# Preparing the second four row tiles over blocks 3 to 7, reordering block 0, and moving one tile pool

## The chip, the cores and the metric

The kernel runs on one core of a Trainium2 chip. The metric is device time in microseconds, as the median of several runs of the whole program. Matrix products run on TensorE (PE in the profile, with PEld for its weight loads), elementwise work on VectorE (DVE), ScalarE (ACT) and GpSimd (POOL); SyncE (SP) issues nearly all DMA transfers. Each engine works through its own list of instructions in order.

## The reference, cut to what matters

One layer of a diffusion backbone: 1024 latent tokens of width 1024 and 256 context tokens, in float32. The inputs are normalised and modulated, multiplied with one combined input matrix of seven blocks of 512 columns, run through retention and differential attention, an output projection and a gated MLP with a depthwise convolution.

```python
m_lat = sc @ w_mod[l] + b_mod[l]                        # 6 x 1024 modulation values
h_lat = rms_norm(x, norm1_g[l]) * (1.0 + sc1) + sh1     # (1024, 1024)
h_ctx = rms_norm(ctx, norm1_g[l]) * (1.0 + csc1) + csh1 # (256, 1024)
... = split_heads(h_lat @ w_in, ...)                    # 7 blocks of 512 columns
...
u = h2 @ w_up ; a, b = split(conv3(u)) ; x = x + g2 * ((silu(a) * b) @ w_down)
return rms_norm(x, final_g)
```

What the change touches is the first part (h_lat, and h_lat times the last 512 columns of w_in), and the place in memory of one tile pool in the product with w_down.

## The kernel before, in words

Tokens are cut into row tiles of 128: eight of the latents (x) and two of the context. Every float32 product is made of three: each operand is split into a high part (rounded) and a low part (the rest), and `passes` (L129 to L134) multiplies high by high (L132), high by low (L133) and low by high (L134).

The first stage (L500 to L718) works on the last block of w_in while its own operands are still being made. The latents are needed transposed and modulated, as hT: for each of eight blocks of 128 columns (d or k = 0 to 7) `modulate` (L544) transposes four row tiles into one PSUM tile (L548), lets ACT write the high part of hT (L551), DVE the exact value (L553) and DVE (even d) or POOL (odd d) the low part (L555). Before that, each row tile has to be loaded (`load_row`, L578), its squares summed on ACT (`square`, L534, L536), the sum raised to the power -1/2 by a small DVE step (L114) and a POOL step (L115) in `power` (L538), and the tile scaled on DVE (`scale`, L541). The modulation values of block d come from w_mod: two pieces of 512 KB are loaded (`mod_load`, five buffers, L512), multiplied on PE (`mod_part`, L520), copied as a row by ACT (`mod_row`, L524) and turned by PE and DVE (`mod_sums`, L530 to L532). The slices of w_in are loaded by `w_load` and split by `w_split` into a high part on ACT (L575) and a low part on DVE (L576). `turn_over(n)` (L591) makes n throw-away products of 128 columns, each two PE instructions, whose result nobody reads.

The rows 0 to 3 (xs0) make the first half of hT, the rows 4 to 7 (xs1) the second. The loop over k (L637) multiplies block k for the row tiles 0 to 3, the first two and the last two apart (`part_products`, L587), and puts the preparation of block k + 2 between. In the kernel before, the second row tiles are loaded in blocks 2 to 5, squared and scaled in blocks 3 to 5, and their latents made in blocks 6 and 7 and at the start of row tile 4. Behind the loop come the stores of row tiles 0 and 1 (`store_to`, two buffers, L394 to L403), and the row tiles 4 and 5 (L712), with the context's preparation put in by `between` (L694). `in_order` (L120, called in L718) fixes the order, as written in the program, of all instructions of PE, DVE, ACT and SP between `begin` and that line. Instructions outside, such as the loads of the rope table (L731) and of the next weights (L186), may be moved in between by the scheduler.

The last stage (from L1330) multiplies the gated hidden tiles (`ghl`, made from stored rows by ACT in L1346 and DVE in L1347) with w_down, whose pieces stay in `resident` tiles (W). The pools of ghl (dop, two buffers of 8 KB a partition) and of the final rows (fin) take memory at the right side, that of W (wres) at the left; memory is reused tile by tile: a new tile waits for the last reader of each old tile that it overlaps. The right side held the tiles of the convolution (`up` in L1204), whose last ones are stored by `down_operands` (L1216; L1220 to L1232, on POOL's queue for the last two blocks). The left side held yT, the operands of the MLP's first product.

Of the kernel before, what the change touches and what calls it, by code (L numbers as in the profile page):

```python
# [17 lines left out]
P = 128  # L18
D = 1024
KD = D // P  # L20
# [52 lines left out]
def kernel(  # L73
# [16 lines left out]
    nc = tc.nc  # L90
    mm = nc.tensor.matmul
# [63 lines left out]
    with ExitStack() as p1:  # L155
# [19 lines left out]

        hT = [[hp.tile([P, KD, 512], F32R, name=f"hT{a}{i}") for i in range(2)] for a in range(2)]
        xs0 = [xr.tile([P, D], F32, name=f"xs{t}") for t in range(4)]
        cT = []
        sm = hp.tile([P, 16], F32, name="sm")
        mcol = hp.tile([P, KD, 2, 2], F32, name="mcol")  # L180
# [33 lines left out]
        def lat_lhs(t, k):  # L214
            return tuple(hT[a][t // 4][:, k, (t % 4) * P : (t % 4 + 1) * P] for a in range(2))
# [284 lines left out]
        with ExitStack() as p0:  # L500
# [61 lines left out]
            def wget(k, c0, c1):  # L562
                return tuple(t[:, k % 2, c0:c1] for t in sl[k // 2])
# [12 lines left out]
                nc.vector.tensor_tensor(out=lo, in0=raw, in1=r32(hi), op=ALU.subtract)  # L576

            def load_row(t):  # L578
                nc.sync.dma_start(out=xs0[t] if t < 4 else xs1[t - 4], in_=x[t * P : (t + 1) * P, :])

            def latents(half, d):
                modulate((xs0, xs1)[half], d, 0, hT[0][half][:, d, :], hT[1][half][:, d, :])
# [2 lines left out]
                modulate(xc, d, 1, cT[0][:, d, :], cT[1][:, d, :])  # L585

            def part_products(ts, k):  # L587
                for t in ts:
                    passes(part[t], lat_lhs(t, k), wget(k, 0, 512), k == 0, k == KD - 1)

            def turn_over(n):  # L591
                for _ in range(n):
# [2 lines left out]
            store = store_to(dv_row, c0=NTC)  # L595
            begin = len(nc.cur_bb.bb.instructions)
            mod_load(0, 0)
            for t in range(3):
                load_row(t)
            mod_load(0, 1)  # L600
            load_row(3)
            w_load(0, 2)
            for q in range(2):
                mod_load(1, q)
            mod_load(2, 0)
            turn_over(4)
            mod_part(0, 0)
            turn_over(10)
            square(xs0[0], 2)
            square(xs0[1], 3)  # L610
            power(2)
# [4 lines left out]
            mod_load(2, 1)  # L616
            w_load(1)
            turn_over(2)
            mod_row(0)
            power(4)  # L620
            scale(xs0[1], 3)
            square(xs0[3], 5)
            mod_sums(0)
            turn_over(4)
            scale(xs0[2], 4)
            power(5)
            w_split(0, 1)
            scale(xs0[3], 5, 0, 2 * P)
            latents(0, 0)
            mod_part(1, 0)  # L630
            mod_part(1, 1)
# [5 lines left out]
            for k in range(KD):  # L637
                part_products((0, 1), k)
                if k == 0:
                    mod_sums(1)  # L640
                    latents(0, 1)
                if k < 2:
                    for q in range(2):
                        mod_part(k + 2, q)
                    mod_row(k + 2)
                if k == 7:
                    latents(1, 2)
                    latents(1, 3)
                if 1 < k < 6:
                    load_row(k + 2)  # L650
                n = k + 4
                if n < KD:
                    for q in range(2):
                        mod_load(n, q)
                if k in (0, 2):
                    w_load(2 + k // 2)
                part_products((2, 3), k)
                if k + 2 < KD:
                    mod_sums(k + 2)
                    latents(0, k + 2)  # L660
                    if 0 < k < 5:
                        for q in range(2):
                            mod_part(k + 3, q)
                        mod_row(k + 3)
                if k in (0, 2, 4):
                    w_split()
                if k == 3:
                    square(xs1[0], 6)
                    power(6)
                if k == 4:  # L670
                    square(xs1[1], 7)
                    scale(xs1[0], 6)
                    power(7)
                if k == 5:
                    first.close()
                    cp = pctx.enter_context(tc.tile_pool(name="cp", bufs=1, side="right"))
                    cT.extend(cp.tile([P, KD, LC], F32R, name=f"cT{a}") for a in range(2))
                    for t in range(NTC):
                        xc.append(xp.tile([P, D], F32, name="xc", tag="wt", bufs=5))
                        nc.sync.dma_start(out=xc[t], in_=ctxt[t * P : (t + 1) * P, :])  # L680
                    square(xs1[2], 8)
                    scale(xs1[1], 7)
                    power(8)
                    square(xs1[3], 9)
                    scale(xs1[2], 8)
                    power(9)
                    scale(xs1[3], 9)
                if k >= 6:
                    latents(1, 4 * (k - 6))
                    latents(1, 4 * (k - 6) + 1)  # L690
            for t in range(2):
                store(t, part[t])

            def between(t, k):  # L694
                if (t, k) == (4, 0):
                    latents(1, 6)
                    latents(1, 7)
                if (t, k) == (4, 1):
                    for i in (2, 3):
                        store(i, part[i])  # L700
# [27 lines left out]

        m2p = m2c.enter_context(tc.tile_pool(name="m2p", bufs=1))
        pad(m2p, 128)  # L730
        rtab = load_rope(1)  # L731
        natural(wget, lat_lhs, range(6, NT), store)
        natural(wget, ctx_lhs, range(NTC), store_to(dv_row))
        wg = stream_block(5)
# [593 lines left out]
    ctx_ya.close()  # L1328

    with ExitStack() as p5:  # L1330
        dop = p5.enter_context(tc.tile_pool(name="dop", bufs=2, side="right", reuse_waits="tile"))
        fin = p5.enter_context(tc.tile_pool(name="fin", bufs=1, side="right", reuse_waits="tile"))
        wres = p5.enter_context(tc.tile_pool(name="wres", bufs=1, reuse_waits="tile"))

# [275 lines left out]
```

## Time and profile before

| | us |
|---|---|
| median of 3 runs | 1405.5 |
| the runs | 1404.98, 1409.08, 1405.5 |
| the profiled execution | 1403.12 |
| its span in the trace | 1401.4 |
| PE busy in the span | 1366.3 (97%) |
| DVE, ACT, POOL busy | 999.9, 729.3, 298.3 |
| DMA moved | 218.81 MB, 156 GB/s |

How to read the rows that follow. A row of the timeline, or of the chain that ended last, has the start in us from the span's start, the duration, the engine, the line of the kernel, the operation, the tile written and those read, the shape and a count of merged instructions; in brackets how long the engine stood before it, and what ended that. Matmuls overlap each other, so the time that one costs is read from start to start. A row of the waits has the total in us, how often and the longest. A row of the windows has the stretch, the busy time and number of instructions of PE, PEld, DVE, ACT and POOL, the clock granted to TensorE (1.00 is full speed), the busy share of the DMA engines and GB/s. A row of the groups has the busy time, the mean of one in ns and the idle time before. Loads issued by SP have no own wait in the chain; a row "DMA xs<-x" is the time from issue to landing.

### The profile page before, as it was taken

The numbers are of one execution on the slowest core, as the hardware profiler recorded it, in microseconds if no ns is written. First come the engines' busy times: TensorE is split into PE (matmuls) and PEld (weight loads), VectorE is DVE, ScalarE is ACT, GpSimd is POOL, SyncE is SP. The second block draws the span as 40 slices with busy tenths as digits, with TensorE's granted clock in tenths as the row PEclk, the third lists the DMA queues.
The fourth block names the chain that finished last, engine by engine and source line by source line (L and its number), as shares of the span: only waits on it lengthen the run. The fifth ranks groups of instructions, "written<-read, shape, count | busy, mean of one in ns | idle before, by whom it ended". The sixth has DMA issues, their size and how long they took to land.

```text
span 1401.4 us, 19449 instructions
## 1 busy us (share of the span) xinstructions
PE 1366.3 (97%) x7040; PEld 1148.0 (82%) x7040; DVE 999.9 (71%) x1458; ACT 729.3 (52%) x1394; POOL 298.3 (21%) x321
## 2 busy tenths in 40 slices
PE   8899999999999899999999999999999999999997
PEld 5688888887887799998888788888888888788886
DVE  3655864423686798896347997887778877699757
ACT  3553313333565589997126655555445555455543
POOL 1310000001556133421201732223332220000001
PEclk9999999999999999999999999999999999999999
DMA  9545885465575696641421223322323325963523
GB/s 337 224 154 196 291 273 190 132 186 174 161 248 154 179 221 156 126 98 46 166 83 60 91 106 113 113 97 106 112 99 113 103 75 180 344 240 101 183 91 127
DMA packets 96807, 218.81 MB, mean 156 GB/s; under 512 B 9220, under 2 KB 31236, under 8 KB 96200
## 3 DMA queue, kind: packets, MB, share of 16 engines
q1 hardware_dynamic: 88408, 192.41, 40.3%
q0 software_dynamic: 8160, 24.91, 7.8%
q8 instruction: 55, 0.90, 0.3%
q14 instruction: 40, 0.33, 0.1%
q10 hardware_dynamic: 144, 0.26, 0.0%
HBM read 160.13 MB, written 57.41 MB: 155 GB/s over the span
## 4 chain that ended last, share of the span: by engine, by line
PE 82%; DVE 7%; DMA 4%; issue 3%; POOL 2%; ACT 2%; SPq 0%; POOLq 0%; ACTq 0%; DVEq 0%
PE chain L132 5%; PE chain L133 5%; PE chain L134 5%; PE pv L872 5%; PE pA L840 5%; PE c L134 4%; PE c L132 4%; PE c L133 4%; PE pn L132 4%; PE pn L134 4%; PE pn L133 4%; PE pl L134 3%; PE third L132 3%; PE third L133 3%; PE pl L132 3%; PE third L134 3%
## 5 line engine op out<-in xcount | busy, mean ns | idle before, releaser
L132 PE MATMUL pl<-hT,whi 128*128 128x512 f32 x256 | 106.2, 415 | 0.0
L132 PE MATMUL chain<-T,whi 128*128 128x512 f32 x264 | 103.2, 392 | 0.8 <-ACT ua L1156 0.5
L133 PE MATMUL chain<-T,whi 128*128 128x512 f32 x264 | 102.8, 389 | 0.0
L134 PE MATMUL chain<-T,wlo 128*128 128x512 f32 x264 | 102.4, 389 | 0.0
L134 PE MATMUL pl<-hT,wlo 128*128 128x512 f32 x256 | 100.3, 392 | 0.1
L133 PE MATMUL pl<-hT,whi 128*128 128x512 f32 x256 | 100.0, 391 | 0.0
L843 DVE TENSOR_REDUCE mt<-pA 128x1 f32<-128x1280 f32 x64 | 95.2, 1490 | 3.7 <-PE pA L840 3.3
L840 PE MATMUL pA<-ks,qhl 128*128 128x512 f32 (+1 forms) x384 | 89.5, 369 | 3.2 <-ACT p L847 3.0
L132 PE MATMUL c<-whi,ghl 128*128 128x512 f32 x232 | 90.4, 390 | 1.4 <-ACT ghl L1346 1.4
L134 PE MATMUL c<-whi,ghl 128*128 128x512 f32 x232 | 90.4, 390 | 0.5 <-DVE ghl L1347 0.5
L133 PE MATMUL c<-wlo,ghl 128*128 128x512 f32 x232 | 90.3, 389 | 0.0
L847 ACT ACTIVATE p<-pA,mt 128x1280 f32<-128x1280 f32 x64 | 85.5, 1335 | 6.7 <-DVE mt L843 6.7
L1011 ACT CAST whi<-cmb 128x512 fp32r<-128x512 f32 x62 | 38.5, 622 | 81.2 <-PE chain L133 60.7
L840 PEld LDWEIGHTS pA<-ks,qhl 128*128 128x128 f32 x384 | 67.6, 189 | 15.5 <-ACT p L847 3.7
L132 PE MATMUL pn<-whi,hT 128*128 128x512 f32 x192 | 79.1, 412 | 0.0
L872 PE MATMUL pv<-va,aT 128*128 128x128 f32 x640 | 77.0, 275 | 0.1
L134 PE MATMUL pn<-whi,hT 128*128 128x512 f32 x192 | 75.6, 394 | 0.9 <-POOL hT L555 0.5
L133 PE MATMUL pn<-wlo,hT 128*128 128x512 f32 x192 | 75.4, 393 | 0.0
L1014 DVE TENSOR_TENSOR wlo<-cmb,whi 128x512 fp32r<-128x512 f32 x62 | 60.5, 976 | 20.3 <-ACT whi L1011 20.3
L872 PEld LDWEIGHTS pv<-va,aT 128*128 128x128 f32 x640 | 74.0, 192 | 0.7 <-DVE yT L901 0.3
L1170 POOL TENSOR_TENSOR cmb<-wrb 128x512 f32<-128x512 f32 x19 | 27.1, 1426 | 221.9 <-DMA wrb<-w_up 159.1
L1011 ACT CAST whi<-wra 128x512 fp32r<-128x512 f32 x55 | 33.7, 622 | 72.9 <-PE third L133 42.6
(313 smaller groups left out, 3819.2 us busy)
## 6 DMA issues: line engine op xcount, KB each, us to landing
wm<-w_mod SPq DMA_DIRECT2D x32, 512.0 KB, 5.3
raw<-w_in SPq DMA_DIRECT2D x27, 512.0 KB, 4.7
wra<-w_up SPq DMA_DIRECT2D x24, 512.0 KB, 3.3
wrb<-w_up SPq DMA_DIRECT2D x22, 512.0 KB, 3.5
W<-w_down SPq DMA_DIRECT2D x44, 256.0 KB, 6.2
ad<-s SPq DMA_DIRECT2D x20, 512.0 KB, 3.4
wra<-ad SPq DMA_DIRECT2D x20, 512.0 KB, 3.4
kvs<-kvg SPq DMA_DIRECT2D x36, 256.0 KB, 3.1
```

Source lines behind the costliest of these rows:

```text
L132: mm(ps, lh, rh, start=first, stop=False, skip_group_check=more)
L133: mm(ps, lh, rl, start=False, stop=False, skip_group_check=more)
L134: mm(ps, ll, rh, start=False, stop=last, skip_group_check=more)
L840: mm(self.pa[m][:, c0:c1], self.q[:, m, i, qs], self.k[:, m, c0:c1], start=(i == 0), stop=(i == 1))
L843: nc.vector.tensor_reduce(out=self.mt[:, m : m + 1], in_=self.pa[m][:, :LK], axis=AX.X, op=ALU.min)
L847: nc.scalar.activation(self.p[m], self.pa[m][:, :LK], AF.Exp, scale=-1.0, bias=self.mt[:, m : m + 1], accum_out=self.s[:, m : m + 1])
L872: mm(self.pv, self.aT[:, c, :], self.v[:, c, :], start=(c == 0), stop=(c == NKT - 1))
L1011: cast = nc.scalar.copy(hi, src)
L1014: nc.vector.tensor_tensor(out=lo, in0=src, in1=r32(hi), op=ALU.subtract)
L1170: nc.gpsimd.tensor_tensor(out=s1, in0=b1, in1=b2, op=ALU.add)
```

## The change

Five things are changed.

1. The loads of the row tiles 0 to 3 are issued by ACT at the very start, instead of by SP between the loads of w_mod.
2. At the start, `turn_over(10)` goes and `turn_over(4)` behind the first `mod_sums` becomes `turn_over(6)`; `mod_row(0)` moves behind the fourth square, the third tile's scaling ahead of `mod_sums(0)`, and the first weight split behind the fourth tile's scaling.
3. In block 0 the third products (low by high) of all four row tiles come behind the first two of all.
4. The second row tiles are loaded in blocks 1 to 4 (ahead of the w_mod pieces of the block), squared in blocks 3 and 4 (ahead of that block's weight split) and scaled in blocks 4 and 5; the latents of the second half are all made in blocks 6 and 7. The rope table's load is put into the fixed order, behind the loop.
5. The pool of ghl moves to the left side, so that W's pool lies behind it and the final rows' pool begins where ghl lay.

```diff
@@ -175,6 +175,8 @@
 
         hT = [[hp.tile([P, KD, 512], F32R, name=f"hT{a}{i}") for i in range(2)] for a in range(2)]
         xs0 = [xr.tile([P, D], F32, name=f"xs{t}") for t in range(4)]
+        for t in range(4):
+            nc.scalar.dma_start(out=xs0[t], in_=x[t * P : (t + 1) * P, :])
         cT = []
         sm = hp.tile([P, 16], F32, name="sm")
         mcol = hp.tile([P, KD, 2, 2], F32, name="mcol")
@@ -576,7 +578,7 @@
                 nc.vector.tensor_tensor(out=lo, in0=raw, in1=r32(hi), op=ALU.subtract)
 
             def load_row(t):
-                nc.sync.dma_start(out=xs0[t] if t < 4 else xs1[t - 4], in_=x[t * P : (t + 1) * P, :])
+                nc.sync.dma_start(out=xs1[t - 4], in_=x[t * P : (t + 1) * P, :])
 
             def latents(half, d):
                 modulate((xs0, xs1)[half], d, 0, hT[0][half][:, d, :], hT[1][half][:, d, :])
@@ -585,8 +587,16 @@
                 modulate(xc, d, 1, cT[0][:, d, :], cT[1][:, d, :])
 
             def part_products(ts, k):
+                if k > 0:
+                    for t in ts:
+                        passes(part[t], lat_lhs(t, k), wget(k, 0, 512), False, k == KD - 1)
+                    return
+                hi, lo = wget(k, 0, 512)
                 for t in ts:
-                    passes(part[t], lat_lhs(t, k), wget(k, 0, 512), k == 0, k == KD - 1)
+                    mm(part[t], lat_lhs(t, k)[0], hi, start=True, stop=False)
+                    mm(part[t], lat_lhs(t, k)[0], lo, start=False, stop=False)
+                for t in range(4) if 3 in ts else ():
+                    mm(part[t], lat_lhs(t, k)[1], hi, start=False, stop=False)
 
             def turn_over(n):
                 for _ in range(n):
@@ -595,17 +605,13 @@
             store = store_to(dv_row, c0=NTC)
             begin = len(nc.cur_bb.bb.instructions)
             mod_load(0, 0)
-            for t in range(3):
-                load_row(t)
             mod_load(0, 1)
-            load_row(3)
             w_load(0, 2)
             for q in range(2):
                 mod_load(1, q)
             mod_load(2, 0)
             turn_over(4)
             mod_part(0, 0)
-            turn_over(10)
             square(xs0[0], 2)
             square(xs0[1], 3)
             power(2)
@@ -616,16 +622,16 @@
             mod_load(2, 1)
             w_load(1)
             turn_over(2)
-            mod_row(0)
             power(4)
             scale(xs0[1], 3)
             square(xs0[3], 5)
+            mod_row(0)
+            power(5)
+            scale(xs0[2], 4)
             mod_sums(0)
-            turn_over(4)
-            scale(xs0[2], 4)
-            power(5)
+            turn_over(6)
+            scale(xs0[3], 5, 0, 2 * P)
             w_split(0, 1)
-            scale(xs0[3], 5, 0, 2 * P)
             latents(0, 0)
             mod_part(1, 0)
             mod_part(1, 1)
@@ -643,11 +649,14 @@
                     for q in range(2):
                         mod_part(k + 2, q)
                     mod_row(k + 2)
-                if k == 7:
-                    latents(1, 2)
-                    latents(1, 3)
-                if 1 < k < 6:
-                    load_row(k + 2)
+                if k == 5:
+                    scale(xs1[2], 8)
+                    scale(xs1[3], 9)
+                if k >= 6:
+                    latents(1, 4 * (k - 6))
+                    latents(1, 4 * (k - 6) + 1)
+                if 0 < k < 5:
+                    load_row(k + 3)
                 n = k + 4
                 if n < KD:
                     for q in range(2):
@@ -662,15 +671,20 @@
                         for q in range(2):
                             mod_part(k + 3, q)
                         mod_row(k + 3)
+                if k == 3:
+                    square(xs1[0], 6)
+                    square(xs1[1], 7)
+                    power(6)
+                    power(7)
+                if k == 4:
+                    scale(xs1[0], 6)
+                    scale(xs1[1], 7)
+                    square(xs1[2], 8)
+                    square(xs1[3], 9)
+                    power(8)
+                    power(9)
                 if k in (0, 2, 4):
                     w_split()
-                if k == 3:
-                    square(xs1[0], 6)
-                    power(6)
-                if k == 4:
-                    square(xs1[1], 7)
-                    scale(xs1[0], 6)
-                    power(7)
                 if k == 5:
                     first.close()
                     cp = pctx.enter_context(tc.tile_pool(name="cp", bufs=1, side="right"))
@@ -678,23 +692,14 @@
                     for t in range(NTC):
                         xc.append(xp.tile([P, D], F32, name="xc", tag="wt", bufs=5))
                         nc.sync.dma_start(out=xc[t], in_=ctxt[t * P : (t + 1) * P, :])
-                    square(xs1[2], 8)
-                    scale(xs1[1], 7)
-                    power(8)
-                    square(xs1[3], 9)
-                    scale(xs1[2], 8)
-                    power(9)
-                    scale(xs1[3], 9)
                 if k >= 6:
-                    latents(1, 4 * (k - 6))
-                    latents(1, 4 * (k - 6) + 1)
+                    latents(1, 4 * (k - 6) + 2)
+                    latents(1, 4 * (k - 6) + 3)
+            rtab = load_rope(1)
             for t in range(2):
                 store(t, part[t])
 
             def between(t, k):
-                if (t, k) == (4, 0):
-                    latents(1, 6)
-                    latents(1, 7)
                 if (t, k) == (4, 1):
                     for i in (2, 3):
                         store(i, part[i])
@@ -728,7 +733,6 @@
 
         m2p = m2c.enter_context(tc.tile_pool(name="m2p", bufs=1))
         pad(m2p, 128)
-        rtab = load_rope(1)
         natural(wget, lat_lhs, range(6, NT), store)
         natural(wget, ctx_lhs, range(NTC), store_to(dv_row))
         wg = stream_block(5)
@@ -1328,7 +1332,7 @@
     ctx_ya.close()
 
     with ExitStack() as p5:
-        dop = p5.enter_context(tc.tile_pool(name="dop", bufs=2, side="right", reuse_waits="tile"))
+        dop = p5.enter_context(tc.tile_pool(name="dop", bufs=2, reuse_waits="tile"))
         fin = p5.enter_context(tc.tile_pool(name="fin", bufs=1, side="right", reuse_waits="tile"))
         wres = p5.enter_context(tc.tile_pool(name="wres", bufs=1, reuse_waits="tile"))
```

## The prediction

> **What bounds the kernel now.** I read the page's busy times first.
>
> ```profile
> PE 1366.3 (97%) x7040; PEld 1148.0 (82%) x7040; DVE 999.9 (71%) x1458; ACT 729.3 (52%) x1394; POOL 298.3 (21%) x321
> ```
>
> TensorE (PE) is busy nearly throughout, so the edits count only where PE stands or runs slowly. The list of PE's waits (us in total, times, longest) names the places that the change touches: the row tiles' transposes (L548), and the gated tiles, which stand further down.
>
> ```profile
> PE pt L548 <- DVE xs L542: 2.0, 2, 1.2
> PE pt L548 <- DVE sm L114: 1.8, 1, 1.8
> ```
>
> The chain and the timeline of the first 20 us (start, duration, engine, line) show what the first product, at 17.98, waits for.
>
> ```profile
> 4.48 9.09 DMA xs<-x
> 13.65 1.15 ACT sq L536 x2
> ...
> 2.12 1.53 SPq L579 DMA_DIRECT2D xs<-x  x3
> 7.21 1.08 PE L520 MATMUL pr<-wt,cz 128*32 128x256 f32 x8 [3.94 <-DMA wt<-w_mod]
> 8.22 4.13 PE L593 MATMUL pn<-ones 128*128 128x128 f32 x20
> 13.03 0.37 ACT L524 COPY rw<-pr 128x256 f32<-128x256 f32 x1 [0.76 <-PE pr L520]
> 13.45 0.61 PE L530 MATMUL pm<-fold,rw 128*128 128x2 f32 x4
> 13.92 1.14 PE L593 MATMUL pn<-ones 128*128 128x128 f32 x8
> 14.89 0.65 PE L548 MATMUL pt<-ident,xs 128*128 128x128 f32 x3
> 17.41 0.64 PE L520 MATMUL pr<-wt,cz 128*32 128x256 f32 x8 [0.16 <-DMA wt<-w_mod]
> 17.98 0.50 PE L132 MATMUL pn<-whi,hT 128*128 128x512 f32 x1
> 18.32 0.40 PE L133 MATMUL pn<-wlo,hT 128*128 128x512 f32 x1
> 19.13 0.50 PE L134 MATMUL pn<-whi,hT 128*128 128x512 f32 x1 [0.41 <-DVE hT L555]
> ...
> 19.87 0.23 PE pn L133
> 20.68 0.49 PE pt L548 x4
> 21.17 1.00 PE pr L520 x16
> ```
>
> Row tile 3 lands at 13.57 (4.48 + 9.09) and is on the chain. The fillers (L593) show a second thing: 20 of them take 4.13 us, 0.21 each, while eight later take 1.14 us, 0.12 from start to start (13.92 to 14.89, where the transposes begin). PE was slow until about 3.4 us into the filler run, and fast behind it.
>
> The same half speed comes back later. In the windows (PE busy, PEld, DVE, ACT, POOL, granted clock, DMA share, GB/s):
>
> ```profile
> 25.00:30.00 5.00, 5.00 (x47) 3.28 (x49) 3.04 (x5) 2.28 (x4) 0.00 (x0) 1.00 0.87 303
> 35.00:40.00 5.00, 5.00 (x41) 3.65 (x38) 3.25 (x6) 2.10 (x3) 0.00 (x0) 1.00 1.03 407
> 50.00:55.00 5.00, 2.01 (x11) 1.32 (x10) 2.50 (x6) 1.54 (x4) 2.78 (x3) 1.00 0.13 52
> 55.00:60.00 5.00, 5.00 (x22) 4.31 (x22) 2.84 (x4) 2.81 (x4) 1.27 (x1) 0.66 0.02 3
> ```
>
> PE stands for 3 of 5 us at 50 to 55, and then gets 0.66 of its clock.
>
> **The change, part by part.** All terms are us of PE time, against the profiled execution.
>
> *Row tiles on ScalarE's (ACT's) queue.* The four loads now leave at 0.7 to 2.5 rather than 2.12 to 5.2, beside SP's instead of between them. The trace has no two hardware queues at once, so I bound. A 512 KB transfer takes 0.524 MB / 407 GB/s (35 to 40) = 1.29 us. Before, six such transfers end with row tile 3 (its three sisters, two pieces of w_mod). If the queues share evenly, six to eight must pass: 0 to +2.5 us. The earlier start takes back up to 1.4 us. So tile 3 lands between 12.2 and 16.1; I keep 13.57, since one more transfer (+1.29) and the earlier start about cancel. ACT's four issues (0.5 each, 1.53 / 3) delay csil by 2 us; that hides behind the first w_mod piece, on which PE waits until 7.21, and would cost the excess only if that piece came under 5 us.
>
> The Trainium skill, page "DMA: Bandwidth & Descriptors", section "Queues, rings and completion order", says that each DMA engine takes turns between the queues, packet by packet; that speaks for even sharing, and no run here shows it yet. By whole-transfer turns tile 3 would come near the early bound, by single rows near the late one.
>
> *Fillers.* Ten (20 products) go, and two are added ahead of the transposes; the moment's row (mod_row) now stands behind the fourth square on ACT. From tile 3's landing: square 1.15, mod_row 0.37, hand-over 0.1, so PE starts the sums 1.6 after it. Then PE has, at full speed, the sums 0.47 (13.45 to 13.92), 12 filler products at 0.12 = 1.45, four transposes 0.5, and two mod_parts, 16 products, 1.0: 3.4 in all. ACT's hT, 1.1 behind the transposes, hides beside the last. But PE was idle or nearly so for most of the time before, and without the ten fillers nothing has made it fast. Bounds: fast at once, 3.4; slow throughout, 6.8. I take slow for 3.4 us as in the filler run: 3.4 + 1.7 = 5.1. First product: 13.57 + 1.6 + 5.1 = 20.3 against 17.98: **+2.3**.
>
> The Trainium skill, "TensorE: Matmul & The Clock Gate", Part 1, states that PE is throttled by default and freed by a busy stretch of a 3.4 us window that runs freely. The trace agrees: 20 slow fillers, then fast. By the page's free phase the slow stretch is 3.4 to 6.8 us, and the first product is 20.3 to 22.0.
>
> *Block 0's low products last.* The first waits for DVE's low half: 19.13 instead of 18.32 + 0.23 = 18.55. Eight high products and block 0's other work now cover it: **-0.6**. The work is the same.
>
> *Second row tiles over blocks 3 to 7.* Rows of the old place:
>
> ```profile
> 45.13 1.05 ACT L575 CAST whi<-raw 128x1024 fp32r<-128x1024 f32 x1
> 46.21 1.23 DVE L576 TENSOR_TENSOR wlo<-raw,whi 128x1024 fp32r<-128x1024 f32 x1
> 48.59 0.39 PE L133 MATMUL pn<-wlo,hT 128*128 128x512 f32 x1
> 53.35 0.33 PE L548 MATMUL pt<-ident,xs 128*128 128x128 f32 x1 [1.84 <-DVE sm L114]
> 54.83 0.77 PE L548 MATMUL pt<-ident,xs 128*128 128x128 f32 x5 [1.15 <-DVE xs L542]
> 63.55 0.66 PE L548 MATMUL pt<-ident,xs 128*128 128x128 f32 x4 [0.68 <-DVE tmp L553]
> 62.67 1.08 ACT L397 ACTIVATE st<-pn 128x512 f32<-128x512 f32 x2
> 63.62 1.47 ACT L551 ACTIVATE hT<-pt,mcol 128x512 fp32r<-128x512 f32 x2
> 69.72 1.58 DVE L542 TENSOR_SCALAR xc<-xc,sm 128x1024 f32<-128x1024 f32 x2 [0.43 <-POOL sm L115]
> ```
>
> With squares and scalings done by block 5, these waits go: 1.84 + 1.15 + 0.68, and the slow stretch that followed, (1 - 0.66) x 5 = 1.7. Sum **-5.4**. A wait for POOL's low half in tile 4 I leave, its queue being the same.
>
> Two things are late next. First, in block 4 the last weight split now stands behind two squares on ACT and their small steps on DVE. Its cast starts 2 x 1.15 after 45.13, at 47.4, ends at 48.5, and the low half is there at 49.75; block 6's second product was due at 48.59: **+1.1**. (All of it shifts with the blocks.) Second, tile 4 no longer waits, so the context rows come late. From the first store on ACT to the second scaled context row took 62.67 to 71.30 = 8.6, with two hT's (1.47) in between that now stand ahead: 7.1 to 8.6. That store starts some 1.2 behind tile 4's first product (those two hT's, less PE's lead). The first context transposes come 30 products, 30 x 0.23 = 7.0, behind it. So 1.3 to 2.8 less what ACT and DVE find free; bounds 0 and 2.8, and I take **+1.7**, near the smaller end, since the old 8.6 held other waits too.
>
> Row tiles 4 to 6 now go ahead of w_mod pieces of their blocks, one transfer more (1.29) in front of the last piece. It costs nothing as long as the queue has room: 25 to 30 moved (407 - 303) x 5 = 0.52 MB too little, one row tile. Without that room, +1.3. The rope table's load moves behind the context rows; its reader comes after 100 us, so nothing.
>
> *Gated tiles' pool.* The memory of ghl:
>
> ```profile
> 1194.89 7.91 DMA ad<-s
> ...
> 1202.86 1.04 ACT L1346 CAST ghl<-wra 128x1024 fp32r<-128x1024 f32 x1 [4.76 <-DMA ad<-s]
> 1203.96 0.50 PE L132 MATMUL c<-whi,ghl 128*128 128x512 f32 x1 [1.38 <-ACT ghl L1346]
> 1205.21 0.50 PE L134 MATMUL c<-whi,ghl 128*128 128x512 f32 x1 [0.53 <-DVE ghl L1347]
> ```
>
> On the right, ghl lies over the last convolution's tiles, whose store lands at 1202.8. On the left it lies over yT, last read before that. ACT was free 4.76 us earlier, so cast (1.04) and subtraction end before PE is ready at 1202.6: **-1.9** (1.38 + 0.53). The bounds are 0 (another late reader lies there) and -1.9. The resident weights move up by 16 KB, over products' operands whose last readers come before their loads by the program's order; nothing, or at most this gain if one load waits.
>
> Sum: +2.3 - 0.6 - 5.4 + 1.1 + 1.7 - 1.9 = **-2.8**. Behind 72 us PE has no wait until the next stages' own, so the shift lasts. The profiled execution took 1403.1 (span 1401.4 and 1.7 around it), the runs' median is 1405.5, 2.4 above; I put the difference on the median: **1402.7**.
>
> **Rivals.**
> 1. *The row tiles come early, PE is fast soon.* Tile 3 at 12.2 and little slow time: first product at 12.2 + 1.6 + 3.4 = 17.2, but the w_mod piece at 17.41 puts it at 18.0 or just under. The +2.3 goes: -5.1, 1400.4; with that piece a transfer earlier, 1399. For it: the loads leave 1.4 to 2.7 us sooner. Against it: PE has little to do before.
> 2. *Slower: PE stays slow through the start.* Tile 3 at 16.1 and slow work throughout, 16.1 + 1.6 + 6.8 = 24.5, +6.5, and block 0's twelve products at half speed, another 12 x 0.23 = 2.8: +9.3 for +2.3, so 1409.7. It decides from a start loss of 5.1 us on. For it: the filler run was there and goes. Against it: the sums to the first product are dense, and a dense run of 3.4 us sufficed before.
> 3. *The spreading doesn't free blocks 6 and 7.* The rows of DVE's two steps of a latent:
>
> ```profile
> L553 DVE TENSOR_SCALAR tmp<-pt,mcol 128x512 f32<-128x512 f32 x16 | 12.8, 806 | 10.1 <-ACT hT L551 10.1
> L555 DVE TENSOR_TENSOR hT<-tmp,hT 128x512 fp32r<-128x512 f32 x8 | 6.2, 781 | 0.3
> ```
>
> For four latents DVE needs 4 x 0.81 + 2 x 0.78 = 4.8 us, PE beside them 12 x 0.23 + 4 x 0.5 = 4.8; with the subtraction of the last split ahead of it DVE may set the pace. Then the 1.84, 1.15 and 0.68 turn into waits for DVE and only the slow stretch goes: +0.9, 1406.4.
>
> **How the numbers follow.** Forecast 0.47, own range 1400.5 to 1405; rival 1 0.25, rival 2 0.13, rival 3 0.15. The bound of 0.3% (4.2 us) is about what a measurement of this kernel can tell from no change. Faster by more (below 1401.3): 0.1 of the forecast's lower end and 0.24 of rival 1, 0.34. Slower by more (above 1409.7): 0.08, of rival 2. Same: 0.58. The range 1398.0 to 1408.5 takes in rivals 1 and 3 and all but rival 2.
>
> **What would show it.** In the new profile: tile 3's landing at 12.2 to 16.1; filler products at 0.21 us ahead of the transposes; the first product near 20.3; no wait for L114 or xs in the second row tiles, and no stretch of 0.66 clock at 55; a wait for wlo in block 6, one for xc before the context; no wait for ghl. I am wrong if PE is fast at the first product, if the store's buffer or DVE holds the late blocks, or if another stage moves.

## The result, and the profile after

The changed kernel took 1399.3 us (median of 15 runs, 1397.68 to 1404.37) beside 1405.5 for the kernel before (15 runs): a ratio of 0.9960, 95% interval 0.9948 to 0.9972. By this ratio, by which all kernels below are compared, it is 5.6 us faster (3.9 to 7.3); the medians themselves differ by 6.2. A second measurement on another occasion (below) gave 0.9975, 0.9965 to 0.9986, so 3.5 less (2.0 to 4.9). The forecast was 2.8 less, 1402.7. Both intervals leave out a ratio of 1; the first lies wholly beyond the forecast gain, the second holds it. The spans of the two profiled executions lie closer together than the medians, 1401.4 before and 1398.8 after.

The page's busy times of the changed kernel:

```profile
PE 1365.4 (98%) x7024; PEld 1145.6 (82%) x7024; DVE 999.9 (71%) x1458; ACT 729.8 (52%) x1394; POOL 297.8 (21%) x321
```

The list of PE's waits (us in total, times, longest), of its first lines those that differ from before:

```profile
PE pr L522 <- DMA wt<-w_mod: 7.5, 2, 6.2
...
PE pt L1062 <- DVE x L1057: 1.4, 1, 1.4
...
PE pn L133 <- DVE wlo L578: 0.8, 1, 0.8
```

The waits for sm, xs and ghl are gone. New are a longer wait for the first w_mod piece, the forecast one for the low weights, and one at L1062, in a stage that the change doesn't touch. The timeline of the start:

```profile
0.74 4.51 ACTq L179 DMA_DIRECT2D xs<-x  x4
9.48 1.08 PE L522 MATMUL pr<-wt,cz 128*32 128x256 f32 x8 [6.21 <-DMA wt<-w_mod]
12.51 1.06 ACT L538 ACTIVATE sq<-xs 128x1024 bf16<-128x1024 f32 x1 [1.62 <-DMA xs<-x]
13.57 0.35 ACT L526 COPY rw<-pr 128x256 f32<-128x256 f32 x1
13.97 1.01 PE L532 MATMUL pm<-fold,rw 128*128 128x2 f32 x4
14.85 2.91 PE L603 MATMUL pn<-ones 128*128 128x128 f32 x12
17.55 1.06 PE L550 MATMUL pt<-ident,xs 128*128 128x128 f32 x4
18.54 1.94 PE L522 MATMUL pr<-wt,cz 128*32 128x256 f32 x16
20.41 0.73 PE L596 MATMUL pn<-whi,hT 128*128 128x512 f32 x1
```

Row tile 3 lands at 12.4 and its square starts at 12.51; before, it landed at 13.57. But twelve filler products take 2.91, 0.24 each, and the four transposes 0.99 from start to start instead of about 0.5: PE is slow all the way to the first product, which comes at 20.41 instead of 17.98. The clock records of the traces say the same: the first record of full clock is at 20.93 us here and at 11.67 before. Of the kernels below, the six profiles with the new start (early fillers among them, rows by SP and fillers kept left out) have PE at full clock from somewhere between 18.16 and 20.93 on, the six with the old start from between 10.18 and 12.93 on.

The windows where PE stood and was then slow before (columns as before):

```profile
50.00:55.00 5.00, 4.24 (x24) 3.23 (x23) 4.58 (x7) 2.64 (x5) 0.61 (x2) 1.00 0.40 122
55.00:60.00 5.00, 4.87 (x28) 3.51 (x27) 4.93 (x7) 3.61 (x6) 2.56 (x2) 1.00 0.35 105
```

PE works 9.1 of these 10 us at full clock. What still stands there is block 6's wait for the low weights (timeline): the split's cast comes behind two squares, as forecast.

```profile
48.21 1.06 ACT L538 ACTIVATE sq<-xs 128x1024 bf16<-128x1024 f32 x1
49.27 1.03 ACT L577 CAST whi<-raw 128x1024 fp32r<-128x1024 f32 x1
50.33 1.23 DVE L578 TENSOR_TENSOR wlo<-raw,whi 128x1024 fp32r<-128x1024 f32 x1 [0.78 <-ACT whi L577]
51.61 0.50 PE L133 MATMUL pn<-wlo,hT 128*128 128x512 f32 x1 [0.76 <-DVE wlo L578]
```

The context's rows (timeline of DVE and PE):

```profile
68.92 0.75 DVE L544 TENSOR_SCALAR xc<-xc,sm 128x1024 f32<-128x1024 f32 x1
70.12 0.75 DVE L544 TENSOR_SCALAR xc<-xc,sm 128x1024 f32<-128x1024 f32 x1 [0.45 <-POOL sm L115]
70.54 0.39 PE L133 MATMUL pn<-wlo,hT 128*128 128x512 f32 x1
70.78 0.27 PE L550 MATMUL pt<-ident,xc 128*128 128x128 f32 x1
```

They are scaled at 70.87 (71.30 before), although PE is further on: 134 products of this stage start ahead of the first transpose here, 126 before. Yet PE waits for nothing. The gated tiles need no wait either: their cast is done ten microseconds ahead of PE.

```profile
1189.10 1.05 ACT L1350 CAST ghl<-wra 128x1024 fp32r<-128x1024 f32 x1 [1.13 <-DMA wra<-ad]
1200.68 0.39 PE L132 MATMUL c<-whi,ghl 128*128 128x512 f32 x1
```

By places, the difference of the two profiled executions is: first product +2.43 (17.98 to 20.41); from there to the next stage's first product -4.51 (80.82 to 76.31); at the start of attention, where PE waits for ACT's probabilities, -1.6; at L1062 +1.9; at the gated tiles -2.4; behind PE's last product, where DVE ends the program, +1.6 (8.47 to 10.10). Sum -2.6. The -1.6 is scatter: the kernel with the pool alone (below), which differs from the one before only behind that place, moves there by +1.7.

The stall at L1062. DVE scales a residual row tile in place (L1057) once its store has landed. The fourth of these in the kernel before, where it is L1053 (timeline of DVE):

```profile
734.18 0.75 DVE L1053 TENSOR_SCALAR x<-x,sm 128x1024 f32<-128x1024 f32 x1 [1.26 <-DMA x1d<-x]
```

The third and fourth in the changed kernel, and PE's transpose that needs the fourth:

```profile
725.05 0.75 DVE L1057 TENSOR_SCALAR x<-x,sm 128x1024 f32<-128x1024 f32 x1 [1.26 <-DMA x1d<-x]
732.73 0.75 DVE L1057 TENSOR_SCALAR x<-x,sm 128x1024 f32<-128x1024 f32 x1 [3.50 <-DMA x1d<-x]
733.54 0.33 PE L1062 MATMUL pt<-ident,x 128*128 128x128 f32 x1 [1.42 <-DVE x L1057]
```

DVE stands 3.50 for the fourth, 1.26 for its sisters. The DMA page of the stretch 726 to 735 (queue, packets, MB, share), and the windows' last two columns, the busy share of the 16 DMA engines and GB/s:

```profile
q1 hardware_dynamic: 144, 0.52, 14.5%
q8 instruction: 1, 0.02, 1.3%
```

```profile
729.00:730.00 1.00, 1.00 (x6) 0.84 (x5) 0.15 (x1) 0.04 (x1) 0.55 (x1) 1.00 0.83 340
730.00:731.00 1.00, 1.00 (x6) 0.81 (x5) 0.00 (x0) 0.00 (x0) 0.00 (x0) 1.00 0.05 8
731.00:732.00 1.00, 1.00 (x7) 0.71 (x5) 0.00 (x0) 0.00 (x0) 0.00 (x0) 1.00 0.05 20
```

One packet of 16 KB of instructions is fetched at 728.7, 0.9 behind the store's issue. When the store's bulk is through, at 730, the share stays near one engine of sixteen (0.05) for two more microseconds. The same happens to the last load of the hidden rows at the very end: 4.53 from issue to landing instead of 2.81, with a fetch 1.9 behind the issue, and ACT waits for it:

```profile
1368.02 0.62 ACT L1015 CAST whi<-wra 128x512 fp32r<-128x512 f32 x1 [2.88 <-DMA wra<-ad]
```

The Trainium skill, "DMA: Bandwidth & Descriptors", section "Queues, rings and completion order", says that the write that counts up a DMA's semaphore lands only after every earlier write of the same DMA engine, across its queues. The trace agrees as far as it goes, and shows more. The 4-byte writes that count up the store's semaphore come fifteen times between 729.89 and 730.04, and once at 732.17. Ahead of this last one, eight 4 KB packets of the store run one after the other from 730.53 on, where the fetch (728.72 to 730.55) ends. So the store's own data stood behind the fetch, not only its count. The trace doesn't name a packet's engine; that it is one of sixteen is read from this order and from the share of 0.05.

### The profile page after: what moved, and what is told of

The parts are those of the page before. It is cut to its first block, busy times and chain, and to the rows that moved or that the text cites. A ratio compares the mean times of both kernels' runs of the same rounds, so it can differ in the third digit from the quotient of the medians.

```text
span 1398.8 us, 19411 instructions
## 1 busy us (share of the span) xinstructions
PE 1365.4 (98%) x7024; PEld 1145.6 (82%) x7024; DVE 999.9 (71%) x1458; ACT 729.8 (52%) x1394; POOL 297.8 (21%) x321
## 4 chain that ended last, share of the span: by engine, by line
PE 81%; DVE 6%; DMA 6%; ACT 2%; issue 2%; POOL 1%; SPq 0%; POOLq 0%; ACTq 0%; DVEq 0%
PE chain L132 5%; PE chain L133 5%; PE chain L134 5%; PE pv L876 5%; PE pA L844 5%; PE c L133 4%; PE c L132 4%; PE c L134 4%; PE pn L132 4%; PE pn L134 4%; PE pn L133 4%; PE third L132 3%; PE third L133 3%; PE third L134 3%; PE pl L134 2%; PE pl L133 2%
## 5 line engine op out<-in xcount | busy, mean ns | idle before, releaser
L132 PE MATMUL pn<-whi,hT 128*128 128x512 f32 x188 | 76.8, 408 | 0.0
L134 PE MATMUL pn<-whi,hT 128*128 128x512 f32 x188 | 73.7, 392 | 0.0
```

Of the source, the lines that this page charges most:

```text
L132: mm(ps, lh, rh, start=first, stop=False, skip_group_check=more)
L134: mm(ps, ll, rh, start=False, stop=last, skip_group_check=more)
```

## The experiments

My theory after the result: the gain is the late rows' and the pool's, with the context's cost covered; the start costs about 2 because PE is slow, and another 3.5 come later from where instruction fetches fall. Rivals: the start is free in the median; the loads on ACT's queue are what is late; the late stalls are accidents. The table gives each kernel's ratio to the kernel before, on the same chip, what that is in us, and of its profile the first product, the way from there to the next stage's first product, DVE's idle time ahead of the fourth scaling, and the last row load from issue to landing.

| kernel | ratio, 95% | us | first product | to next stage | DVE idle | last load |
|---|---|---|---|---|---|---|
| before | 1 | | 17.98 | 80.82 | 1.26 | 2.81 |
| changed | 0.9960 (0.9948 to 0.9972) | -5.6 | 20.41 | 76.31 | 3.50 | 4.53 |
| changed, again | 0.9975 (0.9965 to 0.9986) | -3.5 | 19.33 | 76.03 | 3.21 | 3.81 |
| pool only | 0.9980 (0.9968 to 0.9991) | -2.8 | 19.13 | 80.61 | 1.26 | 2.49 |
| start only | 1.0026 (1.0016 to 1.0037) | +3.6 | 20.02 | 79.98 | 3.38 | 2.49 |
| rows only | 0.9960 (0.9946 to 0.9974) | -5.6 | 18.33 | 76.92 | 1.26 | 2.73 |
| block 0 only | 0.9999 (0.9987 to 1.0012) | -0.1 | 17.99 | 81.22 | 1.25 | 2.54 |
| changed, old start | 0.9939 (0.9923 to 0.9955) | -8.6 | 17.96 | 75.82 | 1.26 | 2.50 |
| early fillers | 0.9942 (0.9929 to 0.9954) | -8.1 | 20.00 | 76.08 | 1.26 | 2.50 |
| fillers kept | 0.9945 (0.9933 to 0.9956) | -7.7 | 18.08 | 76.07 | 1.25 | 4.38 |
| rows by SP | 0.9977 (0.9969 to 0.9986) | -3.2 | 20.39 | 75.87 | 3.22 | 4.38 |
| tile 6 in order | 0.9982 (0.9972 to 0.9991) | -2.5 | 19.98 | 77.94 | 3.45 | 4.67 |
| split first | 0.9972 (0.9961 to 0.9983) | -3.9 | 20.46 | 76.14 | 2.81 | 4.06 |
| old start, split first | 0.9933 (0.9920 to 0.9945) | -9.4 | 17.27 | 75.94 | 1.25 | 2.69 |

**The pool alone**, on the kernel before:

```diff
-        dop = ...tile_pool(name="dop", bufs=2, side="right", reuse_waits="tile")
+        dop = ...tile_pool(name="dop", bufs=2, reuse_waits="tile")
```

> The kernel before with one edit: the pool of ghl on the left side. The sum of places (my theory): the two waits at the gated tiles (1.38 + 0.53 in the profile of before) and some 0.5 more go, and the end of the program, where DVE and not PE is last, gives back up to 1.6: -0.8 to -2.4 against the kernel before. The rival (the end is set by the last loads of the rows and by DVE, not by PE): 0 to -0.3, with the waits gone all the same. In the profile no wait for ghl at 1200 by either; they part in the shift of the last instruction.

Measured -2.8 (-4.5 to -1.3), 0.4 beyond the theory's range, which the interval spans. Between 1202 and 1247 PE gains 2.5 on the kernel before (2.7 behind it at the first, 0.25 at the second) and the wait for ghl is gone; PE's end is 8.46 from the program's end as before, so nothing is given back here. The rival fell.

**The start alone**: edits 1 and 2, block 0 in the old order.

> The kernel before with the start alone edited: the four row tiles loaded by ACT, the fillers cut, the moment's row, the scalings and the weight split in their new order; block 0's products in their old order. My theory: the first product comes at about 20.4 instead of 17.98, because PE works at half speed up to there, and nothing later gives that back: +2.4 against the kernel before (1.5 to 3.5). The rival: the 2.4 of the profiled pair belongs to that one execution's clock windows, and the median moves by less than 0.7 either way. In the profile: 12 products of the fillers ahead of the transposes at 0.24 each by my theory, 0.12 by the rival.

Measured +3.6 (+2.2 to +5.2), at the upper end of the theory's range. The rival fell. The first product comes 2.04 later than before, with the twelve fillers at 0.24; another 2.7 are lost around L1062 (from +1.3 at 723 to +4.0 at 773), where DVE stands 3.38. So the start costs more than its own place shows. The half clock of the old rows is in this kernel too, and where a stretch begins 2 us later it is 55 to 65 (windows):

```profile
55.00:60.00 5.00, 3.75 (x14) 2.90 (x15) 4.20 (x7) 1.45 (x2) 0.56 (x1) 0.73 0.23 78
60.00:65.00 5.00, 4.86 (x31) 4.11 (x30) 3.33 (x6) 3.38 (x6) 2.36 (x2) 0.93 0.08 30
```

**The rows alone**: edit 4 on the kernel before.

> The kernel before with only the second row tiles spread (loads in blocks 1 to 4, squares in 3 and 4, scalings in 4 and 5, latents in 6 and 7, the rope table in the fixed order). My theory: the waits of 1.84, 1.15 and 0.68 and, in the profiled execution, the 1.7 of half clock behind them go, one wait of about 0.8 to 1.1 for the low weights comes in block 6: -4.2 against the kernel before (-3.0 to -5.0). The rival, by which the start is free in the median and the profiled run of before was a short one: -2.5 to -3.0, as only the waits go, the half clock being an accident of that run. A second rival: the change's gain of 5.6 in the medians is all here, -5.5 or more.

Measured -5.6 (-7.6 to -3.6); in the profile the way to the next stage is 3.9 shorter than before and the span 3.4. The value is the second rival's, outside the theory's range of -3.0 to -5.0; the interval holds the theory's -4.2 as well, so the run doesn't part the two. The first rival, -2.5 to -3.0, lies outside it. What the profile settles is the places: no wait for sm, one of 0.8 for the low weights, and no stretch under full clock between 50 and 65. All four profiles with the old rows have such a stretch between 50 and 65, none of the ten with the new rows does.

**The changed kernel with the old start**: edits 1 and 2 undone.

> The changed kernel with the old start: the row tiles loaded by SP between the pieces of w_mod, the ten fillers kept, the old order up to the first latents; block 0's order, the spread row tiles and the pool as changed. My theory: the first product is back at about 18.0 and all later stages come 2.4 earlier, so 2.4 below the changed kernel, about 1396.9 beside its 1399.3 (1.5 to 3.5 below). The rival, by which the start costs nothing in the median: within 0.7 of the changed kernel.

Measured -8.6 (-10.8 to -6.3) against the kernel before, 3 to 5 below the changed kernel's two results. The interval overlaps the first of them (-7.3 to -3.9) and not the second; the old start is compared with the new on one chip further down, under split first. Start +3.6, rows -5.6, pool -2.8, block 0 -0.1: the four parts alone sum to -4.9, between the whole change's two results.

**Eight more fillers at the very start.** They run while PE waits 6.2 for w_mod, and give PE as many fillers as before: 12 + 2 + 6 = 20, where the changed kernel has 4 + 2 + 6 = 12.

```diff
-            turn_over(4)
+            turn_over(12)
             mod_part(0, 0)
```

> The changed kernel with eight more fillers at its very start, where PE waits 6.2 us for the first piece of w_mod: as many PE instructions as before, at a place where they cost nothing. Two later losses of the changed kernel are in question: the wait of 1.4 at L1062 (DVE's scaling 2.2 late behind a store issued at 727.83, with an instruction fetch on one DMA engine at 728.7) and the last load of the rows (4.53 instead of 2.4 from issue to landing, with an instruction fetch at 1365.4). My theory: both come from where the fetches of instructions fall, and that is set by the number of PE instructions ahead; with the old number both go, the first product stays at about 20.4, and the time is 2 to 3.5 below the changed kernel: 1396 to 1397.5 beside its 1399.3. The rival, by which these losses come from the later start or from the loads on ACT's queue: within 0.7 of the changed kernel.

Measured -8.1 (-10.0 to -6.5) against the kernel before, 2.5 to 4.6 below the changed kernel; the interval overlaps the changed kernel's first and not its second. The first product is where it was, at 20.00: by the trace's clock records PE is at full clock from 6.14 to 9.55 only and at half until 19.79. Both late losses are gone:

```profile
730.29 0.76 DVE L1057 TENSOR_SCALAR x<-x,sm 128x1024 f32<-128x1024 f32 x1 [1.26 <-DMA x1d<-x]
```

The last load takes 2.50. At L1062 this kernel shows that the number of PE's instructions decides, as its first product comes no earlier or later than in the changed kernel's two profiles (19.33 and 20.41) and the stall is gone. That it does so through the fetches is what the traces have beside it; no run moves a fetch alone. In the six profiles with twelve fillers a fetch starts 0.7 to 1.0 behind the fourth store's issue and DVE stands 2.81 to 3.50; in the other eight it lies 1.7 to 2.7 ahead of it and DVE stands 1.25 or 1.26. For the last load it is less strict: six of seven with a fetch 0.9 to 2.0 behind the issue take 3.81 to 4.67, but the start-only kernel's takes 2.49; the kernel with the fillers kept (below) is among the six. What a late load costs is plain: in the six profiles that have it the program ends 9.37 to 10.21 behind PE's last product, in the other eight 8.46 to 8.48.

**The ten fillers kept**, two ahead of the transposes, the rows loaded by ACT:

```diff
             mod_part(0, 0)
+            turn_over(10)
...
-            turn_over(6)
+            turn_over(2)
```

> The changed kernel, its row tiles loaded by ACT, with the ten fillers kept at their old place and two instead of six ahead of the transposes. My theory (PE's half speed and not the loads makes the start late): PE is fast from the fillers' end, the first product comes at 18.2 to 18.8, 1.6 to 2.2 earlier; with only two fillers fewer than before, the fetches fall nearly as before and the wait at L1062 goes: 3 to 4.2 below the changed kernel. The rival (the loads on ACT's queue are what is late, as the first piece of w_mod lands 2.2 later): first product at 20 or later, within 1 of the changed kernel, or as far below it as the kernel with early fillers.

Measured -7.7 (-9.4 to -6.2), 2.1 to 4.2 below the changed kernel's two results. The rival fell. The first product comes at 18.08 behind the same late w_mod piece (timeline):

```profile
10.67 3.72 PE L603 MATMUL pn<-ones 128*128 128x128 f32 x20
14.89 0.71 PE L603 MATMUL pn<-ones 128*128 128x128 f32 x4
15.92 0.69 PE L603 MATMUL pn<-ones 128*128 128x128 f32 x4
16.45 0.70 PE L550 MATMUL pt<-ident,xs 128*128 128x128 f32 x4
18.08 0.50 PE L596 MATMUL pn<-whi,hT 128*128 128x512 f32 x1
```

PE is busy from 10.67 on and at full speed by 14.9: four filler products in 0.71, where the slow ones of the changed kernel take 0.24 each. The wait at L1062 is gone; the late load (4.38) is not, as a fetch lies 1.9 behind its issue.

**The rows loaded by SP**, fillers as changed:

```diff
             mod_load(0, 0)
+            for t in range(3):
+                load_row(t)
             mod_load(0, 1)
+            load_row(3)
```

> The changed kernel with the row tiles loaded by SP between the pieces of w_mod as before, the fillers as changed. My theory: the first piece of w_mod is back at 7.2, but PE is slow as in the changed kernel, so the first product comes at 19.5 to 20.5 and the time is within 1 of the changed kernel (0 to 0.9 below). The rival (the loads on ACT's queue are what is late): first product at 18 to 18.5, 2 below the changed kernel.

Measured -3.2 (-4.3 to -2.0) against the kernel before. The first product comes at 20.39 with the fillers at 0.24 again (timeline):

```profile
15.63 2.91 PE L601 MATMUL pn<-ones 128*128 128x128 f32 x12
```

That the ACT queue's loads are what is late fell. The time is 0.3 and 2.4 above the changed kernel's two results, where I had expected it 0 to 0.9 below; the interval overlaps both, so no difference is shown.

**Row tiles 6 and 7 inside the fixed order**, that is, behind the context's transposes in PE's list:

```diff
-            in_order(begin)
...
         natural(wget, lat_lhs, range(6, NT), store)
+        in_order(begin)
```

> The changed kernel with row tiles 6 and 7 inside the fixed order, so that none of row tile 6's products can stand ahead of the context's transposes. In the changed kernel ten of them do, in the kernel before one. My theory: the scaled context rows are as late as was forecast (+1.7), and the forecast cost did not come because these ten products, 10 x 0.23 = 2.3, fill the time; without them PE waits 1.7 to 2.3 for xc at about 69, and the time is that much above the changed kernel: 1401.0 to 1401.6 beside its 1399.3. The rival (the context rows are early enough, or the wait is made up before the next stage): within 0.5 of the changed kernel.

Measured -2.5 (-3.9 to -1.3) against the kernel before, 1.0 to 3.1 above the changed kernel's two results; the interval overlaps that of the second. The profile is clearer. The way to the next stage is 77.94, 1.9 longer than the mean of the others with the new rows and block 0's order (76.03), and the waits from 60 to 80 us name the cause:

```profile
PE pt L550 <- DVE xc L544: 1.5, 2, 0.8
```

At its place the rival fell: the context's rows are late, and in the changed kernel products of row tile 6 hide it.

**The weight split ahead of the squares** in block 4:

```diff
+                if k in (0, 2, 4):
+                    w_split()
                 if k == 3:
                     square(xs1[0], 6)
...
-                if k in (0, 2, 4):
-                    w_split()
```

> The changed kernel with the weight split of block 4 ahead of that block's squares and scalings instead of behind them. My theory: the wait of 0.8 for the low weights in block 6 goes, the squares come 1.1 later and nothing waits for them, since the tiles' first transposes come two blocks later: 0.8 below the changed kernel. The rival (the squares are late then, and the wait moves to the transposes of blocks 6 and 7): within 0.3 of it, with PE waiting for xs or sm.

Measured -3.9 (-5.5 to -2.4); the changed kernel beside it -3.5. The wait for the low weights goes and one of 0.5 for xs comes (waits, 45 to 70 us):

```profile
PE pt L550 <- DVE xs L544: 0.5, 1, 0.5
```

The rival's mechanism is right: 76.14 to the next stage is no less than without it. Beside the changed kernel on the same chip the median is the same, 1400.61 and 1400.59. The 0.8 is not to be had by this alone.

**Old start and split first**:

> The changed kernel with the old start and the weight split first in block 4: all that has shown a gain so far, together. The sum of the places: 8.6 below the kernel before for the old start with the rest of the change, and another 0.8 for the split: a ratio of 0.993 to 0.9935. The rival, that the split's place is covered or the instructions' fetches fall worse: no better than 0.9939, the ratio with the old start alone.

Measured -9.4 (-11.2 to -7.7), the fastest of all. It differs from the split-first kernel by the start alone, and ran on the same chip: the median is 1395.23 beside 1400.61, 5.4 less, and the intervals of the two ratios are apart. In the profiles the first product is 3.2 earlier, the stall at L1062 1.6 shorter and the end 1.1 nearer to PE's last product. The split's own part isn't shown: to the next stage it is 75.94 beside 75.82 without it, and the intervals overlap.

**Block 0's order alone**:

> The kernel before with block 0's third products behind the first two of all four row tiles, and nothing else. My theory: the wait of 0.41 for DVE's low half goes, block 0 is 0.5 shorter in the profile, and the time is 0.5 below the kernel before, less than the runs can tell from nothing. The rival (PE waits elsewhere for the same low half, or for block 1): 0.

Measured -0.1 (-1.8 to +1.7), which tells nothing apart by itself. In the profile block 0 is 0.65 to 0.69 ahead from 24 to 47 us; by 59 that is lost, as the half clock lasts longer than before (windows):

```profile
50.00:55.00 5.00, 2.01 (x10) 1.43 (x9) 1.83 (x5) 1.23 (x3) 2.41 (x3) 0.84 0.00 0
55.00:60.00 5.00, 5.00 (x19) 4.22 (x17) 2.45 (x4) 2.21 (x4) 1.27 (x1) 0.50 0.02 3
```

That is (0.16 + 0.50) x 5 = 3.3 us at stake beside 1.7 before.

**The changed kernel once more**, unaltered:

> The changed kernel once more, unaltered, beside the others on one chip, with a second profile. If the two late losses come from where the instruction fetches fall, they stand in this profile as in the first: PE's wait at L1062 of 1.4 with DVE 3.5 idle, and the last load at about 4.5. If they were accidents of the first execution, at least one of them is gone. First product at 20 to 20.4. Ratio to the kernel before 0.995 to 0.997 as measured first.

Measured -3.5 (-4.9 to -2.0). Both late losses stand again (DVE 3.21 idle, the last load 3.81), so they are no accidents. The first product came at 19.33, a little ahead of what was expected, PE being at full clock from 18.16 on (20.93 in the first execution).

## Why the prediction was right or wrong

The sum was -2.8; the runs gave -3.5 and -5.6. Size and sign are right, and the gain is larger than the sum by one term that didn't come, and smaller than it could be by one mechanism that wasn't seen.

- **The start, +2.3.** Six profiles with the old start have their first product at 18.11 on average (17.27 to 19.13), six with the changed one at 20.03 (19.33 to 20.46; early fillers among them, rows by SP left out): +1.9. The size is right by luck, as two errors cancel. Row tile 3 came some 1.1 earlier than the 13.57 that I kept, so in these six PE began the sums at 13.88 to 14.12 and not at 15.2. From there to the first product it took 5.3 to 6.4 us, not 5.1, because it was slow nearly all the way and not for 3.4 us. ACT's four issues, put at 0.5 each, took 4.51 in all; that cost nothing, as PE waits for w_mod until 9.48. Rival 1 had the first half, rival 2 the second; neither came as a whole.
- **Block 0, -0.6.** 0.65 at its place; not measurable in the whole.
- **The late rows, -5.4.** The waits of 1.84, 1.15 and 0.68 and the half clock are gone. DVE did not become the bound: rival 3 fell, PE waits for no latent in blocks 6 and 7.
- **The weight split, +1.1.** It is 0.8, at the place and for the reason given.
- **The context, +1.7.** This is the step that failed. That the rows would come late is right: with row tile 6 held back, PE waits and 1.9 are lost. But row tiles 6 and 7 stand outside the fixed order, and the scheduler put ten of tile 6's products (one in the kernel before) ahead of the second transpose, eight of them ahead of the first. I had counted 30 products between tile 4's start and the transposes; there are ten more, 10 x 0.23 = 2.3. With that term at 0, rows and block 0 give -4.9 instead of -3.2, and the runs show -4.4 (80.47, the mean of three with the old rows, to 76.03).
- **The pool, -1.9.** 2.4 to 2.5 at its place, -2.8 as a median. The two waits that were summed went, and PE gained 0.5 more than they; where that lies was not tried. The traces have one thing more: in two of the four profiles with the old pool (rows alone, block 0 alone) PE runs at half clock for 3.41 us behind these waits and reaches its end 1.6 later for it, and in none of the ten with the new pool. So the pool may spare more than the waits in some executions; that is read from few profiles and not shown. The stretch in the kernel with the rows alone (windows):

```profile
1200.00:1205.00 5.00, 4.79 (x14) 3.83 (x15) 3.69 (x6) 2.53 (x5) 0.00 (x0) 0.66 0.74 227
```

- **Not in the sum: the number of PE's instructions.** With eight fillers fewer a fetch of instructions falls on the store at 728 and on the load at 1363: +1.9 and +1.6 in the first profile. I had counted the fillers as PE time only. Without it the change is worth about 8, as the kernel with early fillers shows.

The range, 1398.0 to 1408.5, held the median. Within 0.3% was called likeliest; the first measurement says faster by 0.4%, the second by 0.25%, so the bound lies between them.

The Trainium skill, "TensorE: Matmul & The Clock Gate", Part 1, states that the window which frees PE runs freely, so that the slow stretch varies. The runs agree: the changed kernel's first product comes at 20.41 in one execution and at 19.33 in the other, with full clock from 20.93 and from 18.16 on.

## What to carry to other kernels

When work is forecast to be late, look in the program for instructions that the scheduler may move into the gap, by name and number, before the gap is priced. Fillers that keep TensorE fast are worth their place only if they end close to the work that they are for: the eight added ones, ending at 6.5 us, left the first product at 20.00, while the ten kept ones, ending at 14.4, brought it to 18.08. Whoever adds or removes instructions should look once more at the whole trace, since places far behind can lose or win two microseconds by it. Parts are best measured alone: here one part cost 3.6, two gained 8.4, and the whole showed only the difference.

## What the runs showed of the hardware that was not expected

- A fetch of 16 KB of instructions, 0.7 to 1.0 us behind the issue of a 512 KB store, held the store's landing by 1.6 to 2.2 us (DVE idle for 2.81 to 3.50 instead of 1.25), six times out of six.
- ACT's four loads took 4.51 us to issue (0.74 to 5.25), but the first three of them 0.40 to 0.46 each, as SP's do. The fourth left at 4.92, when the first had landed (4.89): in the trace both count on the same semaphore.
- The clock column says 1.00 from 10 to 20 us in the changed kernel, though its fillers take 0.24; its trace has no clock record before 20.93. With the early fillers the same twelve take 2.91 as well, and there the column has values (windows of the kernel with early fillers):

```profile
10.00:15.00 5.00, 3.73 (x26) 2.33 (x19) 1.90 (x6) 2.80 (x6) 2.03 (x3) 0.50 1.03 415
15.00:20.00 5.00, 5.00 (x32) 3.55 (x31) 1.83 (x5) 0.78 (x1) 0.00 (x0) 0.52 1.00 410
```

So at a program's start, ahead of the first clock record, a filler's duration is the better witness than the column.
